# A lookup's gate matrices with their columns in one run, and the end of the kernel dealt with token block by token block

## The chip, the cores and the metric

The kernel runs on one NeuronCore of a Trainium2 chip. The metric is device time in microseconds (us) of one execution. Five engines with their own instruction queues work side by side and wait for one another by semaphores: TensorE (PE; its weight loads are shown apart as PEld), VectorE (DVE), ScalarE (ACT), GpSimd (POOL) and SyncE (SP), which here issues all loads. Tiles have 128 partitions; on-chip memory is SBUF, and matrix products are collected in PSUM.

## The reference

256 tokens of width 1024 pass a block of two layers and then a second block. Each layer of the first block has a mixer and a lookup feed-forward over 16384 small experts, a 128 by 128 grid. Cut to what matters:

```python
def peer(xn, w_q, sub_keys, u, v):                 # 256 tokens, 8 heads
    q = (t @ w_q).reshape(n_tok, 8, 2, 128)
    sc = jnp.einsum('thpd,hpnd->thpn', q, sub_keys)
    s1, i1 = lax.top_k(sc[:, :, 0], 16); s2, i2 = lax.top_k(sc[:, :, 1], 16)
    cand = s1[..., :, None] + s2[..., None, :]     # 16 x 16 candidates
    top_s, pos = lax.top_k(cand, 16)
    eidx = (i1 * 128 + i2) at pos                  # 8 x 16 = 128 picks per token
    gate = softmax(top_s)
    hid = gelu(einsum('td,thkd->thk', t, u[eidx]))
    return einsum('thk,thkd->td', gate * hid, v[eidx])
```

The second block ends in a mixture of 32 experts (four groups of eight, two of the eight chosen per token), a layer norm, a gated projection (`sigmoid(x @ ple_gate) * (p @ ple_proj)`) added to the residual stream, and a last layer norm.

## The kernel before, in words

A product of two fp32 matrices is made of three: each side is split into a high part (a cast on ACT) and a rest (a subtraction on DVE), both in a rounded fp32 format; hi·hi, lo·hi and hi·lo are added in PSUM. `split` (L98) does this, `wload` (L105) loads 128x1024 weights and splits them into `whi` and `wlo`, and `mm` (L119) issues every matmul.

The lookup does not gather. It computes the hidden value of every expert for every token and multiplies by a gate matrix that is zero except at the 128 picks of a token. `H[i2, i1, token]` holds it in three fp32 tiles (rows i1 0 to 63, 64 to 95, 96 to 127), each `[128, rows, 256]`, so that two neighbouring rows i1 of one token lie 1024 bytes apart. A loop over 128 rows i1 runs 24 matmuls `ph` each (8 x 3, moving 256 tokens), puts gelu(ph) into the row (tokens whose gate is already there are multiplied by it on DVE, L784; the others are written by ACT, L780), and from about the fortieth row on deals with groups of four tokens as its rate `due` allows: 64 groups spread over the remaining rows, so about two groups in three rows.

For one group, `build` makes two f16 tiles on DVE, with the 128 picks of a token on the partitions. `pab` holds two one-hot matrices (does pick k have i1 = n? i2 = n?) for four tokens, laid out `[128, 2, 128 values, 4 tokens]`: the token is the last index, so the 128 values of one token lie 8 bytes apart. `pgb` is the i2 one-hot times the gate, in a high and a low f16 part, in the same layout. Per token two matmuls follow (`gates`): the weights are a part of `pgb`, the moving side is the i1 one-hot, both read with that step of 8 bytes, and the sum of the two lands in 128 columns of a PSUM tile `g` of 512. Then `g` is taken out, one instruction for each of the three H tiles: rows with hidden values present are multiplied on DVE (L764, at the same time by 1/GATE_UNIT), the rest are written by ACT (L767); the elements go token by token and within a token along the rows.

What feeds `build` is `IT`, the transposed picks: two indices and the two gate parts, `[128, 4, 256]`, written once per layer by `to_picks` (L694 to L697) behind a search for the best sixteen on DVE. It runs over the first rows of the same loop.

The order on each engine is set by a scheduler that simulates the program, under pools of buffers; the helper `behind` adds an order dependence on one engine.

The last part: the 32 experts end with `ea` matmuls whose results are split into `yc` (L98). Then a branch runs an overflow path where a group has over 128 tokens; two numbers are read into registers ahead of it (`values_load`, L1537 and L1538), on every engine. Behind the branch, 32 `sc` matmuls put the experts' rows back in token order for the two token blocks t0 and t1, DVE adds the residual into `y` (L1552), and a layer norm (`Ln`) follows: statistics, a reciprocal root by a chain of small instructions (L167 to L182), two passes over the data (L317, L319), transposes `tp` (L204) and a split of what they give (`xh`, `xl`). Then `out_proj` runs 96 matmuls `o` against `ple_gate`, whose weights (`o00` to `o03`, `o10` to `o13`: half, quarter) are loaded and split behind the branch, and `sink` (L1584 to L1586), a last `Ln` and four stores end the program.

Of the kernel before, what the change touches and what calls it, by code (L numbers as in the profile page):

```python
# [8 lines left out]
F32 = mybir.dt.float32  # L9
# [44 lines left out]
def program(tc, A, out, stop=None, start=None):  # L54
# [16 lines left out]
    tinyp = ctx.enter_context(pool("tinyp", 3))  # L71
# [305 lines left out]
    def out_proj(wpool, src, xT, sink, order=(0, 1, 2, 3), both=1):  # L377
# [21 lines left out]
        for t in range(2):  # L399
            for n in range(2):  # L400
                for g in order[both:]:
                    if t == 0:
                        late[n, g] = wload(src[n, g], wpool, f"o{n}{g}")
                    block(late[n, g], g, n, t)
                sink(t, n, os_[t][n])
# [166 lines left out]
    def peer(l, xT, make):  # L572
        with ExitStack() as es:
# [4 lines left out]
            IT = pip.tile([P, 4, S], F16, tag="IT", name="IT")  # L578
            iota4 = pip.tile([P, P, 4], F16, tag="iota4", name="iota4")
            ACT.copy(iota4, iota[:, :, None].to_broadcast([P, P, 4]))  # L580
# [108 lines left out]
            def to_picks():  # L689
                for t in range(2):  # L690
# [4 lines left out]
                    ts = slice(t * P, (t + 1) * P)  # L695
                    V.tensor_copy(IT[:, 0:3, ts], ps[:, :384].rearrange("p (i t) -> p i t", i=3))
                    V.tensor_tensor(IT[:, 3, ts], ps[:, S:S + P], IT[:, 2, ts], op=ALU.subtract)  # L697

# [42 lines left out]
            def build(grp):  # L741
                ts = slice(4 * grp, 4 * grp + 4)
                ab = pw.tile([P, 2, P, 4], F16, tag="pab", name="pab", bufs=2)
                V.tensor_tensor(ab, iota4[:, None, :, :].to_broadcast([P, 2, P, 4]),  # L744
                                IT[:, 0:2, ts][:, :, None, :].to_broadcast([P, 2, P, 4]), op=ALU.is_equal)
                b = pw.tile([P, 2, P, 4], F16, tag="pgb", name="pgb", bufs=2)
                V.tensor_tensor(b, ab[:, 1:2, :, :].to_broadcast([P, 2, P, 4]),  # L747
                                IT[:, 2:4, ts][:, :, None, :].to_broadcast([P, 2, P, 4]), op=ALU.mult)
                built[grp] = ab, b

            def gates(grp, n):
                t0 = 4 * grp
                ab, b = built.pop(grp)
                ps = smt("g")
                for i in range(4):
                    for part in range(2):
                        mm(ps[:, i * P:(i + 1) * P], b[:, part, :, i], ab[:, 0, :, i], part == 0, part == 1)
                pv = ps.rearrange("p (t i) -> p t i", t=4)
                for o, end, part in parts:
                    size = end - o  # L760
                    hv = part[:, :, t0:t0 + 4].rearrange("p i t -> p t i")
                    m = min(max(n - o, 0), size)
                    if m:
                        V.scalar_tensor_tensor(hv[:, :, :m], hv[:, :, :m], 1.0 / GATE_UNIT, pv[:, :, o:o + m],  # L764
                                               op0=ALU.mult, op1=ALU.mult)
                    if m < size:
                        ACT.activation(hv[:, :, m:], pv[:, :, o + m:end], AF.Copy, scale=1.0 / GATE_UNIT)  # L767
# [61 lines left out]
            for t in range(2):  # L829
                for n in range(2):  # L830
                    for i1, w, v in held:
                        value_block(i1, w, v, t, (n,))
                    V.tensor_tensor(h[:, t, half(n)], h[:, t, half(n)], acc[t][n], op=ALU.add)
# [461 lines left out]
    def moe(x):  # L1295
        xT, (carry, (rs, rb, iota1), products), xn = x
        pp = ctx.enter_context(pool("pp")).tile([P, 2, D], F32, tag="pp", name="pp")
        with ExitStack() as es:
# [89 lines left out]
            wr = es.enter_context(pool("mwr", RAWS))  # L1388
# [50 lines left out]
            yc, accs = {}, {}  # L1439
# [10 lines left out]
            def overflow():  # L1450
# [27 lines left out]
                for e in range(8):  # L1478
                    pu = up(lambda q: A["exp_gu_g"][bass.ds(group, 1), e, q].rearrange("a p c -> (a p) c"),
                            [[x[:, k, :] for k in range(DK)] for x in xo])  # L1480
                    hT = middle(pu, co[:, e:e + 1])
                    down(lambda f: A["exp_down_g"][bass.ds(group, 1), e, f].rearrange("a p c -> (a p) c"),
# [43 lines left out]
            before = None  # L1526
# [220 lines left out]
```

## Time and profile before

| | us |
|---|---|
| three runs | 2632.81, 2632.82, 2633.84 |
| median | 2632.82 |
| the profiled execution's own time | 2631.19 |
| its span in the profile | 2629.4 |
| PE busy (matmul) | 2554.3 |
| DVE busy | 1929.9 |
| ACT busy | 1362.3 |

The page sums busy time over the whole program, so its shares are means over stages. The views beneath are read stage by stage: windows (busy time in a stretch), groups of instructions by shape (count, mean length), and timelines (start, length and count of neighbouring instructions of one kind). A matmul's length in a timeline reaches past the start of the next one, as they overlap in the array; what a matmul costs is the distance from start to start. The first lookup's gates stand between 305 and 621 us, the second's between 1254 and 1571 us, and the last part begins at about 2571 us.

### The profile page before, as it was taken

To read this page: it belongs to the slowest core of one execution; us is meant where nothing else is said; L and a number is where in the kernel's file an instruction comes from. 1 tells how busy PE (TensorE), PEld (TensorE's weight loads), DVE (VectorE), ACT (ScalarE), POOL (GpSimd) and SP (SyncE) were. 2 spreads that over 40 slices of the span, in tenths; PEclk is the share of its full clock that TensorE was granted. 3 is DMA by queue.
4 is the path that set the end of the run, shared out by engine and by line. 5 is a ranking of instruction groups with operands and counts; after the bars stand their busy time and mean duration, and the time that the engine had idled before them with its cause. 6 is when DMAs were issued, how large, how long until landed. Compare 5 with 4: busy or idle time off the path is not lost. (4 is left out here: it accounts for less than half of the span.)

```text
span 2629.4 us, 42151 instructions
## 1 busy us (share of the span) xinstructions
PE 2554.3 (97%) x16202; PEld 2288.0 (87%) x16202; DVE 1929.9 (73%) x3548; ACT 1362.3 (52%) x2315; POOL 3.3 (0%) x24
## 2 busy tenths in 40 slices
PE   8999999999999999999999999999999999899996
PEld 7899999998888889899999998888878899688885
DVE  6689877887555556799878885555567566799997
ACT  5555655444444444555554444444456433478872
POOL 0000000000000000000000000000000000000000
PEclk9999999999999999999999999999999999899998
DMA  6445444444555554555444445555644214599983
GB/s 210 162 137 184 163 151 149 152 150 161 191 186 190 186 200 152 172 167 184 148 150 153 153 149 182 190 186 195 205 162 132 77 61 142 204 351 351 353 320 113
DMA packets 131777, 474.74 MB, mean 181 GB/s; under 512 B 15218, under 2 KB 16242, under 8 KB 131314
## 3 DMA queue, kind: packets, MB, share of 16 engines
q1 hardware_dynamic: 131570, 472.00, 52.8%
q8 instruction: 128, 2.10, 0.3%
q14 instruction: 79, 0.65, 0.1%
HBM read 470.89 MB, written 1.05 MB: 179 GB/s over the span
## 5 line engine op out<-in xcount | busy, mean ns | idle before, releaser
L98 DVE TENSOR_TENSOR wlo<-raw,whi 128x1024 fp32r<-128x1024 f32 x738 | 902.1, 1223 | 512.3 <-ACT whi L98 481.1
L98 ACT CAST whi<-raw 128x1024 fp32r<-128x1024 f32 x738 | 775.2, 1051 | 871.1 <-PE acc L119 349.9
L119 PE MATMUL ph<-xh,whi 128*128 128x256 f32 x2048 | 511.8, 288 | 0.0
L119 PE MATMUL ph<-xl,whi 128*128 128x256 f32 x2048 | 501.4, 282 | 0.0
L119 PE MATMUL acc<-whi,hw 128*128 128x512 f32 x1952 | 496.5, 396 | 2.4 <-ACT hw L98 2.2
L119 PEld LDWEIGHTS acc<-whi,hw 128*128 128x128 f32 x1952 | 366.7, 188 | 91.9 <-ACT hw L98 2.6
L119 PEld LDWEIGHTS ph<-xh,whi 128*128 128x128 f32 x2048 | 392.6, 192 | 0.1
L119 PEld LDWEIGHTS ph<-xl,whi 128*128 128x128 f32 x2048 | 391.6, 191 | 0.0
L119 PE MATMUL ph<-xh,wlo 128*128 128x256 f32 x2048 | 287.2, 283 | 0.0
L119 PE MATMUL acc<-wlo,hw 128*128 128x512 f32 x976 | 267.9, 396 | 0.0
L119 PEld LDWEIGHTS ph<-xh,wlo 128*128 128x128 f32 x2048 | 264.1, 192 | 0.0
L119 PEld LDWEIGHTS acc<-wlo,hw 128*128 128x128 f32 x976 | 183.5, 188 | 44.2
L119 PE MATMUL g<-pab,pgb 128*128 128x128 f16 x1024 | 140.6, 296 | 0.0
L98 DVE TENSOR_TENSOR mlo<-raw,mhi 128x1024 fp32r<-128x1024 f32 x96 | 116.7, 1223 | 10.9 <-ACT mhi L98 8.1
L764 DVE SCALAR_TENSOR_TENSOR H<-H,g 128x256 f32<-128x256 f32 (+26 forms) x254 | 120.9, 515 | 0.5 <-PE g L119 0.4
L767 ACT ACTIVATE H<-g 128x128 f32<-128x128 f32 (+20 forms) x254 | 67.9, 360 | 99.5 <-DVE H L764 99.5
L98 ACT CAST mhi<-raw 128x1024 fp32r<-128x1024 f32 x96 | 100.9, 1053 | 25.1 <-PE gu L119 19.4
L119 PEld LDWEIGHTS <-pgb 128*128 128x128 f16 x1024 | 105.0, 118 | 6.5
L747 DVE TENSOR_TENSOR pgb<-pab,IT 128x1024 f16<-128x1024 f16 x128 | 87.5, 688 | 1.9
L744 DVE TENSOR_TENSOR pab<-iota,IT 128x1024 f16<-128x1024 f16 x128 | 87.2, 682 | 0.0
L98 DVE TENSOR_TENSOR hw<-H,hw 128x512 fp32r<-128x512 f32 x128 | 87.1, 684 | 0.0
L780 ACT ACTIVATE H<-ph 128x256 f32<-128x256 f32 (+40 forms) x254 | 78.2, 308 | 12.0 <-PE ph L119 11.9
(676 smaller groups left out, 3599.0 us busy)
## 6 DMA issues: line engine op xcount, KB each, us to landing
raw<-in_peer_u SPq DMA_DIRECT2D x256, 512.0 KB, 3.3
raw<-in_peer_v SPq DMA_DIRECT2D x256, 512.0 KB, 4.2
raw<-in_exp_gu SPq DMA_DIRECT2D x128, 512.0 KB, 5.3
raw<-in_exp_down SPq DMA_DIRECT2D x64, 512.0 KB, 5.2
raw<-in_peer_w_q SPq DMA_DIRECT2D x32, 512.0 KB, 3.3
raw<-in_even_w_in SPq DMA_DIRECT2D x28, 512.0 KB, 4.2
raw<-in_odd_w_in SPq DMA_DIRECT2D x24, 512.0 KB, 3.8
raw<-in_w_in_g SPq DMA_DIRECT2D x16, 512.0 KB, 3.3
```

What stands on the lines that cost most here:

```text
L98: return ACT.copy(hi, src), V.tensor_tensor(lo, src, hi, op=ALU.subtract)
L119: i = nc.tensor.matmul(o, l, r, start=start, stop=stop)
L744: V.tensor_tensor(ab, iota4[:, None, :, :].to_broadcast([P, 2, P, 4]), IT[:, 0:2, ts][:, :, None, :].to_broadcast([P, 2, P, 4]), op=ALU.is ...
L747: V.tensor_tensor(b, ab[:, 1:2, :, :].to_broadcast([P, 2, P, 4]), IT[:, 2:4, ts][:, :, None, :].to_broadcast([P, 2, P, 4]), op=ALU.mult)
L764: V.scalar_tensor_tensor(hv[:, :, :m], hv[:, :, :m], 1.0 / GATE_UNIT, pv[:, :, o:o + m], op0=ALU.mult, op1=ALU.mult)
L767: ACT.activation(hv[:, :, m:], pv[:, :, o + m:end], AF.Copy, scale=1.0 / GATE_UNIT)
L780: ACT.activation(hrow[:, tk:], ph[:, tk:S], AF.Gelu)
```

## The change

The gate side of the lookup is laid out token by token. `IT` becomes `[128, 64 groups, 4, 4 tokens, 2]` with each value stored twice, `iota4` becomes a plain row of 128 numbers, and `pab` is `[128, 2, 4 tokens, 128 values]`, so that a token's 128 columns are one run of 256 bytes. The gate now multiplies the i1 one-hot, the side that moves, and the weights are the bare i2 one-hot; there are still two products per token. The multiplication that made `pgb` is two instructions of 512 elements in place of one of 1024. `g` is taken out with rows as the outer and tokens as the inner index, so that H is touched in runs of four words and PSUM with a step of 512 bytes. The factor 1/GATE_UNIT moves to the add that ends the lookup. `to_picks` writes each value twice, by three copies and a subtraction of 256 elements per token block, in place of one copy of 384 and a subtraction of 128. Tiny tiles have two buffers in place of three.

In the last part the registers are loaded, in program order, ahead of expert (3, 0); the first two `ple_gate` weights (`a0`, `a1`) are loaded and split in front of the branch and the next two right behind it; the layer norm runs with `in_turn`, so that t1's residual add waits for t0's last pass; and `out_proj` takes those weights as they are.

```diff
@@ -68,7 +68,7 @@
     wp = ctx.enter_context(pool("wp", 2))
     hp = ctx.enter_context(pool("hp", 1))
     xp = ctx.enter_context(pool("xp", 1))
-    tinyp = ctx.enter_context(pool("tinyp", 3))
+    tinyp = ctx.enter_context(pool("tinyp", 2))
     mm_ps = ctx.enter_context(tc.tile_pool(name="mm_ps", bufs=2, space=PSUM))
     sm_ps = ctx.enter_context(tc.tile_pool(name="sm_ps", bufs=4, space=PSUM))
@@ -400,7 +400,7 @@
             for n in range(2):
                 for g in order[both:]:
                     if t == 0:
-                        late[n, g] = wload(src[n, g], wpool, f"o{n}{g}")
+                        late[n, g] = ready[n, g] if (n, g) in ready else wload(src[n, g], wpool, f"o{n}{g}")
                     block(late[n, g], g, n, t)
                 sink(t, n, os_[t][n])
@@ -575,9 +575,10 @@
             pw = es.enter_context(pool("pw", 4))
             pip = es.enter_context(pool("pi"))
             last = hbp.tile([P, 32, S], F32, tag="last", name="H")
-            IT = pip.tile([P, 4, S], F16, tag="IT", name="IT")
-            iota4 = pip.tile([P, P, 4], F16, tag="iota4", name="iota4")
-            ACT.copy(iota4, iota[:, :, None].to_broadcast([P, P, 4]))
+
+            IT = pip.tile([P, 64, 4, 4, 2], F16, tag="IT", name="IT")
+            iota1 = pip.tile([P, P], F16, tag="iota1", name="iota1")
+            ACT.copy(iota1, iota)
             h0es = ExitStack()
             h0p = h0es.enter_context(pool("h0"))
             mid = h0p.tile([P, 32, S], F32, tag="mid", name="H")
@@ -692,9 +693,12 @@
                     for i in range(3):
                         nc.tensor.transpose(ps[:, i * P:(i + 1) * P],
                                             res[:, i, t, :, :].rearrange("p h k -> p (h k)"), ident)
-                    ts = slice(t * P, (t + 1) * P)
-                    V.tensor_copy(IT[:, 0:3, ts], ps[:, :384].rearrange("p (i t) -> p i t", i=3))
-                    V.tensor_tensor(IT[:, 3, ts], ps[:, S:S + P], IT[:, 2, ts], op=ALU.subtract)
+                    o = IT[:, 32 * t:32 * t + 32]
+                    pv = [ps[:, i * P:(i + 1) * P].rearrange("p (g t) -> p g t", t=4)[:, :, :, None]
+                          .to_broadcast([P, 32, 4, 2]) for i in range(3)]
+                    for i in range(3):
+                        V.tensor_copy(o[:, :, i], pv[i])
+                    V.tensor_tensor(o[:, :, 3], pv[2], o[:, :, 2], op=ALU.subtract)
             steps = [first_level(t, c) for c in range(16) for t in range(2)]
             for t in range(2):
@@ -739,32 +743,36 @@
             built = {}
             def build(grp):
-                ts = slice(4 * grp, 4 * grp + 4)
-                ab = pw.tile([P, 2, P, 4], F16, tag="pab", name="pab", bufs=2)
-                V.tensor_tensor(ab, iota4[:, None, :, :].to_broadcast([P, 2, P, 4]),
-                                IT[:, 0:2, ts][:, :, None, :].to_broadcast([P, 2, P, 4]), op=ALU.is_equal)
-                b = pw.tile([P, 2, P, 4], F16, tag="pgb", name="pgb", bufs=2)
-                V.tensor_tensor(b, ab[:, 1:2, :, :].to_broadcast([P, 2, P, 4]),
-                                IT[:, 2:4, ts][:, :, None, :].to_broadcast([P, 2, P, 4]), op=ALU.mult)
-                built[grp] = ab, b
+
+
+                it = IT[:, grp].rearrange("p r t k -> p (r t) k")[:, :, None, :]
+                ab = pw.tile([P, 2, 4, P], F16, tag="pab", name="pab", bufs=2)
+                V.tensor_tensor(ab.rearrange("p r t (i k) -> p (r t) i k", k=2),
+                                iota1.rearrange("p (i k) -> p i k", k=2)[:, None, :, :].to_broadcast([P, 8, 64, 2]),
+                                it[:, 0:8].to_broadcast([P, 8, 64, 2]), op=ALU.is_equal)
+                g = pw.tile([P, 4, 2, P], F16, tag="pgb", name="pgb", bufs=2)
+                for r in range(2):
+                    V.tensor_tensor(g[:, :, r, :].rearrange("p t (i k) -> p t i k", k=2),
+                                    ab[:, 0].rearrange("p t (i k) -> p t i k", k=2),
+                                    it[:, 8 + 4 * r:12 + 4 * r].to_broadcast([P, 4, 64, 2]), op=ALU.mult)
+                built[grp] = ab, g
             def gates(grp, n):
+
                 t0 = 4 * grp
-                ab, b = built.pop(grp)
+                ab, g = built.pop(grp)
                 ps = smt("g")
                 for i in range(4):
-                    for part in range(2):
-                        mm(ps[:, i * P:(i + 1) * P], b[:, part, :, i], ab[:, 0, :, i], part == 0, part == 1)
-                pv = ps.rearrange("p (t i) -> p t i", t=4)
+                    for r in range(2):
+                        mm(ps[:, i * P:(i + 1) * P], ab[:, 1, i, :], g[:, i, r, :], r == 0, r == 1)
+                pv = ps.rearrange("p (t i) -> p i t", t=4)
                 for o, end, part in parts:
-                    size = end - o
-                    hv = part[:, :, t0:t0 + 4].rearrange("p i t -> p t i")
-                    m = min(max(n - o, 0), size)
-                    if m:
-                        V.scalar_tensor_tensor(hv[:, :, :m], hv[:, :, :m], 1.0 / GATE_UNIT, pv[:, :, o:o + m],
-                                               op0=ALU.mult, op1=ALU.mult)
-                    if m < size:
-                        ACT.activation(hv[:, :, m:], pv[:, :, o + m:end], AF.Copy, scale=1.0 / GATE_UNIT)
+                    hv = part[:, :, t0:t0 + 4]
+                    m = min(max(n, o), end)
+                    if m > o:
+                        V.tensor_tensor(hv[:, :m - o], hv[:, :m - o], pv[:, o:m], op=ALU.mult)
+                    if m < end:
+                        ACT.copy(hv[:, m - o:], pv[:, m:end])
             grp, due = 0, 0.0
             for i1 in range(NK):
@@ -830,7 +838,8 @@
                 for n in range(2):
                     for i1, w, v in held:
                         value_block(i1, w, v, t, (n,))
-                    V.tensor_tensor(h[:, t, half(n)], h[:, t, half(n)], acc[t][n], op=ALU.add)
+                    V.scalar_tensor_tensor(h[:, t, half(n)], acc[t][n], 1.0 / GATE_UNIT, h[:, t, half(n)],
+                                           op0=ALU.mult, op1=ALU.add)
                     if nxt:
                         nxt.half(t, n)
             return nxt.late() if nxt else None
@@ -1523,9 +1533,13 @@
                 V.tensor_copy(flag[:, 0:1], c8[:, 0:1])
                 V.tensor_copy(flag[:, 1:2], ci[:, 0:1])
-            before = None
+            before, vals = None, []
             for g in range(4):
                 for e in range(8):
+                    if (g, e) == (3, 0):
+                        vals += [nc.values_load(flag[0:1, 0:1], min_val=0, max_val=256),
+                                 nc.values_load(flag[0:1, 1:2], min_val=0, max_val=3)]
+                        nonlocal_group[:] = vals[1:]
                     pu = up(lambda q: A["exp_gu"][8 * g + e, q], [[x[:, k, g, :] for k in range(DK)] for x in xc])
                     if before is None:
                         with tc.issue_after(gathered.ins):
@@ -1534,24 +1548,32 @@
                         finish_expert(*before)
                     before = (e, g, middle(pu, cw[:, g, e:e + 1]))
             finish_expert(*before)
-            vals = nc.values_load(flag[0:1, 0:1], min_val=0, max_val=256), \
-                nc.values_load(flag[0:1, 1:2], min_val=0, max_val=3)
-            group = vals[1]
+
+            ahead = {}
+            for g in range(2):
+                raw = rawp.tile([P, 1024], F32, tag="raw", name="raw")
+                nc.sync.dma_start(raw, A["ple_gate"][0, g])
+                ahead[0, g] = [wr.tile([P, 1024], F32R, tag="raw", name=f"a{g}") for _ in range(2)]
+                split(raw, *ahead[0, g])
+            rooms[:] = [(0, rawp, "raw")] * 4
             with tc.If(vals[0] > P):
                 overflow()
+            for g in range(2, 4):
+                ahead[0, g] = wload(A["ple_gate"][0, g])
             gb_ = st([P, 2, D], "gb", tag="xc0")
             for i in range(2):
                 nc.sync.dma_start(gb_[:, i, :], A[f"lnr2{i}"].partition_broadcast(P))
-            ln = Ln([y[:, t, :] for t in range(2)], [gb_[:, i, :] for i in range(2)])
+            ln = Ln([y[:, t, :] for t in range(2)], [gb_[:, i, :] for i in range(2)], in_turn=True)
             for t in range(2):
                 for n in range(2):
                     ps = mmt("sc")
                     for g in range(4):
                         for i in range(2):
                             mm(ps, selT[:, g, t * P:(t + 1) * P], yc[g][i][:, half(n)], g == 0 and i == 0, g == 3 and i == 1)
-                    V.scalar_tensor_tensor(y[:, t, half(n)], h[:, t, half(n)], ALPHA, ps, op0=ALU.mult, op1=ALU.add)
+                    with behind(ln.done):
+                        V.scalar_tensor_tensor(y[:, t, half(n)], h[:, t, half(n)], ALPHA, ps, op0=ALU.mult, op1=ALU.add)
                     ln.half(t, n)
-            return ln.xT, pp
+            return ln.xT, pp, ahead, own
     def ple_products(ep):
```

On DVE, in the first lookup at rows i1 of about 93, a stretch of the loop read as follows before (`wlo` is the split of the loop's weights, `ge` the gelu of tokens already gated):

```order
L764 SCALAR_TENSOR_TENSOR H<-H,g 128x4x64
L764 SCALAR_TENSOR_TENSOR H<-H,g 128x4x29
L784 TENSOR_TENSOR H<-H,ge 128x160
L744 TENSOR_TENSOR pab<-iota_1365,IT 128x1024
L747 TENSOR_TENSOR pgb<-pab,IT 128x1024
L98 TENSOR_TENSOR wlo<-raw,whi 128x1024
L764 SCALAR_TENSOR_TENSOR H<-H,g 128x4x64
```

The same stretch now:

```order
L773 TENSOR_TENSOR H<-H,g 128x64x4
L773 TENSOR_TENSOR H<-H,g 128x29x4
L792 TENSOR_TENSOR H<-H,ge 128x160
L750 TENSOR_TENSOR pab<-iota_1365,IT 128x1024
L755 TENSOR_TENSOR pgb<-pab,IT 128x4x128 x2
L98 TENSOR_TENSOR wlo<-raw,whi 128x1024
L773 TENSOR_TENSOR H<-H,g 128x64x4
```

Nothing has moved there: one instruction of `pgb` has become two, and `H<-H,g` has rows outside and four tokens inside.

On PE, where the first gates of the first lookup begin (`it` is a transpose of `to_picks`), the rows before were the following:

```order
L119 MATMUL ph<-xl,whi 128x256
L119 MATMUL ph<-xh,wlo 128x256 x8
L119 MATMUL ph<-xh,whi 128x256
...
L119 MATMUL ph<-xl,whi 128x256
L119 LDWEIGHTS pgb
L119 MATMUL g<-pab,pgb 128x128
L119 LDWEIGHTS pgb
L119 MATMUL g<-pab,pgb 128x128
```

And now:

```order
L694 MATMUL it<-ident,H 128x128
L119 MATMUL ph<-xh,wlo 128x256 x8
L119 LDWEIGHTS pab
L119 MATMUL g<-pgb,pab 128x128
L119 MATMUL ph<-xh,whi 128x256
...
L119 MATMUL ph<-xl,whi 128x256
L119 LDWEIGHTS pab
L119 MATMUL g<-pgb,pab 128x128
L119 MATMUL ph<-xh,whi 128x256
L119 MATMUL ph<-xl,whi 128x256
L119 LDWEIGHTS pab
L119 MATMUL g<-pgb,pab 128x128
```

A single pair of a gate's weight load and matmul now stands ahead of the next row's 24 `ph` matmuls, a second one (of another group) within them, and the gates' roles as weights and moving side are exchanged.

On DVE behind the branch (the last part's layer norm) before, from the first residual add on:

```order
L1552 SCALAR_TENSOR_TENSOR y_24052<-h,sc 128x512
L300 BN_STATS lst<-y_24052 128x6
L1552 SCALAR_TENSOR_TENSOR y_24052<-h,sc 128x512
L300 BN_STATS lst<-y_24052 128x6
L303 BN_AGGR lmv<-lst 128x2
L1552 SCALAR_TENSOR_TENSOR y_24052<-h,sc 128x512
L312 TENSOR_SCALAR lv<-lmv 128x1
L317 SCALAR_TENSOR_TENSOR y_24052<-y_24052,lmv,gb 128x512 x2
L300 BN_STATS lst<-y_24052 128x6
L171 TENSOR_SCALAR rsi<-lv 128x1
L1552 SCALAR_TENSOR_TENSOR y_24052<-h,sc 128x512
```

And now:

```order
L1574 SCALAR_TENSOR_TENSOR y_24188<-h,sc 128x512
L300 BN_STATS lst<-y_24188 128x6
L98 TENSOR_TENSOR wlo<-raw,whi 128x1024
L1574 SCALAR_TENSOR_TENSOR y_24188<-h,sc 128x512
L98 TENSOR_TENSOR wlo<-raw,whi 128x1024
L300 BN_STATS lst<-y_24188 128x6
L303 BN_AGGR lmv<-lst 128x2
...
L317 SCALAR_TENSOR_TENSOR y_24188<-y_24188,lmv,gb 128x512 x2
L319 SCALAR_TENSOR_TENSOR h<-y_24188,lr,gb 128x512 x2
L1574 SCALAR_TENSOR_TENSOR y_24188<-h,sc 128x512 x2
L300 BN_STATS lst<-y_24188 128x6
```

Before, t1's adds and statistics stand between the steps of t0's norm. Now t0's norm runs to its end (L319), and t1's adds come behind it.

On PE the `o` matmuls of the two token blocks were mixed, behind all transposes:

```order
L119 MATMUL sc<-yc_26782,selT 128x512
L204 MATMUL tp<-ident,h 128x128 x16
L119 MATMUL o_27711<-o00hi,xh 128x512
L119 MATMUL o_27711<-o00hi,xl 128x512
L119 MATMUL o_27711<-o00hi,xh 128x512
L119 MATMUL o_27711<-o00hi,xl 128x512
L119 MATMUL o_27713<-o00hi,xh 128x512
L119 MATMUL o_27713<-o00hi,xl 128x512
```

Now t0's transposes are followed by t0's first half (24 matmuls) before those of t1:

```order
L119 MATMUL sc<-yc_26946,selT 128x512
L204 MATMUL tp<-ident,h 128x128 x8
L119 MATMUL o_27870<-a_26953,xh 128x512
L119 MATMUL o_27870<-a_26953,xl 128x512
...
L119 MATMUL o_27870<-wlo,xh 128x512 x2
L204 MATMUL tp<-ident,h 128x128 x8
L119 MATMUL o_27871<-o10hi,xh 128x512
L119 MATMUL o_27871<-o10hi,xl 128x512
```

The transposes of t1 have moved behind the 24 matmuls of t0's first half. The loads into registers, on the other hand, stand directly in front of the branch on PE, ACT and DVE as before.

## Rows read from the trace of the kernel before

**Rows 1.** The page: busy time by engine, and the granted clock in 40 slices.
```profile
PE 2554.3 (97%) x16202; PEld 2288.0 (87%) x16202; DVE 1929.9 (73%) x3548; ACT 1362.3 (52%) x2315; POOL 3.3 (0%) x24
...
PEclk9999999999999999999999999999999999899998
```

**Rows 2.** Windows in the two lookups; per engine busy us (count), granted clock, DMA share, GB/s.
```profile
300.00:400.00 100.00, 100.00 (x840) 99.04 (x839) 77.25 (x131) 53.02 (x147) 0.00 (x0) 1.00 0.44 148
...
500.00:600.00 100.00, 100.00 (x840) 98.93 (x839) 86.19 (x150) 43.10 (x105) 0.00 (x0) 1.00 0.45 152
1100.00:1200.00 100.00, 100.00 (x841) 100.00 (x841) 94.00 (x388) 52.03 (x83) 0.00 (x0) 1.00 0.53 173
```

**Rows 3.** Groups by shape, whole run: busy us, mean ns | idle before.
```profile
L119 PE MATMUL g<-pab,pgb 128*128 128x128 f16 x1024 | 140.6, 296 | 0.0
...
L119 PEld LDWEIGHTS <-pgb 128*128 128x128 f16 x1024 | 105.0, 118 | 6.5
...
L747 DVE TENSOR_TENSOR pgb<-pab,IT 128x1024 f16<-128x1024 f16 x128 | 87.5, 688 | 1.9
L744 DVE TENSOR_TENSOR pab<-iota,IT 128x1024 f16<-128x1024 f16 x128 | 87.2, 682 | 0.0
...
L764 DVE SCALAR_TENSOR_TENSOR H<-H,g 128x256 f32<-128x256 f32 x86 | 64.2, 746 | 0.0
...
L767 ACT ACTIVATE H<-g 128x128 f32<-128x128 f32 x132 | 46.7, 431 | 8.9 <-DVE H L764 8.9
```

**Rows 4.** Timeline of PE, 400 to 410 us: start, length, line, operation, count.
```profile
403.08 1.12 PE L119 MATMUL ph<-xh,wlo 128*128 128x256 f32 x8
404.05 1.11 PE L119 MATMUL g<-pab,pgb 128*128 128x128 f16 x8
404.91 0.37 PE L119 MATMUL ph<-xh,whi 128*128 128x256 f32 x1
```

**Rows 5.** Timeline of PE in the last part, idle before and what ended it.
```profile
2587.45 1.94 PE L204 MATMUL tp<-ident,h 128*128 128x128 f32 x8 [5.61 <-DVE h L319]
...
2598.58 0.40 PE L119 MATMUL o<-o01hi,xh 128*128 128x512 f32 x1
2598.81 0.40 PE L119 MATMUL o<-o01hi,xl 128*128 128x512 f32 x1
```

**Rows 6.** Timeline of PE, 2100 to 2106 us: full fp32 with 128 columns.
```profile
2103.52 1.05 PE L119 MATMUL i<-XT,it 128*128 128x128 f32 x8
2104.41 1.06 PE L119 MATMUL i<-it,XT 128*128 128x128 f32 x8
```

**Rows 7.** Timeline of weight loads, 402.5 to 405 us.
```profile
402.97 1.03 PEld L119 LDWEIGHTS ph<-xh,wlo 128*128 128x128 f32 x8
404.04 0.82 PEld L119 LDWEIGHTS <-pgb 128*128 128x128 f16 x8
```

**Rows 8.** Groups by shape on DVE, 300 to 640 us.
```profile
L764 DVE SCALAR_TENSOR_TENSOR H<-H,g 128x128 f32<-128x128 f32 x23 | 10.1, 438 | 0.2 <-PE g L119 0.2
...
L696 DVE CAST IT<-it 128x384 f16<-128x384 f32 x1 | 0.6, 558 | 0.1
...
L784 DVE TENSOR_TENSOR H<-H,ge 128x256 f32<-128x256 f32 x1 | 0.4, 420 | 0.0
L684 DVE TENSOR_TENSOR H<-H 128x512 bf16<-128x512 bf16 x1 | 0.4, 413 | 0.0
```

**Rows 9.** Lines 1343 (comparison that repeats one word) and 697: ns min/median/max.
```profile
L1343 DVE TENSOR_TENSOR sel<-iota,key x2: 673/682/692, 2279.1 to 2282.4; 128x512 fp32r<-128x512 f32 x2
...
L697 DVE TENSOR_TENSOR IT<-it,IT x4: 280/284/286, 298.0 to 1264.1; 128x128 f16<-128x128 f32 x4
```

**Rows 10.** Chain that ended last, in order of time: start, us, what.
```profile
2586.59 1.38 DVE h L319 x2
...
2592.49 24.92 PE o L119 x96
...
2619.41 1.41 DVE y L319 x2
```

More of the change, by code (lines that the diff above doesn't have):

```diff
@@ L375, in fresh, with out_proj @@
             return nxt.late()
-    def out_proj(wpool, src, xT, sink, order=(0, 1, 2, 3), both=1):
+    def out_proj(wpool, src, xT, sink, order=(0, 1, 2, 3), both=1, ready=()):
         os_ = [[mmt(f"o{t}{n}") for n in range(2)] for t in range(2)]
@@ L1387, in moe @@
             y = late.tile([P, 2, D], F32, tag="y2", name="y2")
-            wr = es.enter_context(pool("mwr", RAWS))
+            own = ExitStack()
+            wr = own.enter_context(pool("mwr", RAWS, side="right"))
             turn = [0]
@@ L1437, in down @@
                                first and f == 0 and i == 0, last and f == 1 and i == 2)
-            yc, accs = {}, {}
+            yc, accs, nonlocal_group = {}, {}, []
             def finish_expert(e, g, hT):
@@ L1478, in overflow @@
                 for e in range(8):
-                    pu = up(lambda q: A["exp_gu_g"][bass.ds(group, 1), e, q].rearrange("a p c -> (a p) c"),
+                    pu = up(lambda q: A["exp_gu_g"][bass.ds(nonlocal_group[0], 1), e, q].rearrange("a p c -> (a p) c"),
                             [[x[:, k, :] for k in range(DK)] for x in xo])
                     hT = middle(pu, co[:, e:e + 1])
-                    down(lambda f: A["exp_down_g"][bass.ds(group, 1), e, f].rearrange("a p c -> (a p) c"),
+                    down(lambda f: A["exp_down_g"][bass.ds(nonlocal_group[0], 1), e, f].rearrange("a p c -> (a p) c"),
                          hT, acc, e == 0, e == 7)
@@ L1575, in ple @@
     def ple(x):
-        xT, pp = x
+        xT, pp, ahead, own = x
         with pool("pl") as ep, pool("plo") as wo, pool("plw", 2) as ew:
@@ L1587, in sink @@
                 ln.half(t, n)
-            out_proj(wo, A["ple_gate"], xT, sink, both=0)
+            out_proj(wo, A["ple_gate"], xT, sink, both=0, ready=ahead)
+        own.close()
     def after(name, x):
@@ L1618, in program @@
                     evacuated[:] = split(h[:, t, :], *[a[:, t, :] for a in xn])
-            xT = (xT, pre, xn) if origin == "ln1" else (xT, pp)
+            xT = (xT, pre, xn) if origin == "ln1" else (xT, pp, {}, ExitStack())
         after(origin, xT)
```

## The prediction

> **What bounds the kernel now.** I read the page's busy line and the slices first: PE is busy 2554.3 of 2629.4 us at a granted clock of nine tenths or more in nearly every slice, DVE 73%, ACT 52% [rows 1]. So work that PE loses comes off the end, as long as nothing else becomes the bound there. [...] In 1100 to 1200 us, the search for the best picks, DVE is at 94.00 and PE still at 100.00: up to that share DVE does not hold PE up [rows 2]. Then the groups by shape: 1024 gate matmuls, with nothing idle ahead of them [rows 3]. Last the timelines, for what one of them costs.
>
> **The gate matmuls.** Eight of them last 1.11 us and one 0.296 [rows 3, 4], so one starts (1.11 − 0.296)/7 = 116 ns after the other. All 1024 take 119 us. The `ph` matmuls ahead of them move 256 columns and need (404.05 − 403.08)/8 = 121 ns each [rows 4]; those of the last part move 512 and need 230 ns [rows 5]. From 121 and 230, 128 columns should cost 121 − 109/2 = about 66 ns; in proportion to 256 it would be 60. Before, the 128 columns cost what 256 do. Two things may be the cause. One is the moving side's step of 8 bytes; the change takes it away. The other is the weight load. Full fp32 with 128 columns runs at (2104.41 − 2103.52)/8 = 111 ns [rows 6], which is close; but eight fp32 loads at a pitch of 121 ns end 1.03 us after the first began, so one lasts about 1.03 − 7 x 0.121 = 0.18 us, against 118 ns for one of f16 [rows 3, 7]: the f16 load should not need the room of an fp32 one. Both sides are contiguous now, so either cause goes unless the load has a price of its own. I take 64 ns: 1024 x (116 − 64) = 53 us less. Bounds from rows: 60 ns (57 us less) and 116 (nothing).
>
> [...]
>
> **What DVE pays per group.** `pab` stays one instruction of 1024 f16 elements (682 ns [rows 3]). Its operands now repeat pairs in place of running over four tokens; a comparison that repeats one word over 512 fp32 elements costs 682 ns [rows 9], much as any of that size, so I count nothing. The bounds are 0 and, if repeated pairs ran at half speed, +0.35 us. `pgb` goes from one instruction of 688 ns to two of 512 elements; 512 two-byte elements cost 413 [rows 8], so 2 x 413 − 688 = +0.14 us per group. Taking `g` out costs 746 ns for 256 elements and 438 for 128 [rows 3, 8], 2.41 ns an element, where the contiguous multiplication of `H` by `ge` needs 420 for 256 [rows 8]. H now comes in runs of four words, PSUM with a step of 512 bytes, which no row shows. The lower bound is 420; above there is no row that ends it, so I keep 746 (the nearest: same operands, one of them strided) and put the dearer case among the rivals. ACT's part (431 ns for 128 [rows 3]) lies on an engine half idle, and costs nothing up to twice that.
>
> [...]
>
> Does DVE still keep up? Three rows of `ph` and two groups make a period of 3 x 24 x 0.120 + 2 x 8 x 0.116 = 10.5 us; now 16 x 0.052 = 0.83 us less, 9.7. DVE in 500 to 600 us works 86.19% [rows 2], 9.05 us per period, plus 2 x 0.14 = 9.3: 96%, just above what was seen to be harmless. In 300 to 400 it is (8.1 + 0.3)/9.7 = 87%. So I count 4 us of small waits over the late half of both lookups.
>
> **The rest of the lookup.** `to_picks` per token block goes from 558 ns [rows 8] plus a subtraction of 284 [rows 9] to four instructions of 256 elements at 420: +0.84 us, four blocks in all, while DVE is near the 94% of rows 2; at worst 3.4 us, none if the search has slack. I take 1.5. The first runs of gates now have single pairs between `ph` matmuls of the row before; PE works in order, so if `pgb` of that group is late, all `ph` behind it wait. Before, the gates came in whole blocks later. A `pab` and a `pgb` last 1.4 us [rows 3]; with one such wait in each lookup that is about 2 us once part of it is hidden, bounds 0 and (two in each) 5. The final add by 1/GATE_UNIT is as long as the plain one: nothing. The third tiny buffer is used by no chain that runs beside two others here: nothing, or some tenths where a norm waits.
>
> **The last part.** The register loads have not moved in the executed order, so that edit is worth nothing. The two early weight splits lie under the last expert's `ea` matmuls, and so are hidden; without cover they would cost 2 x 1.05 us on ACT. `in_turn` makes t0's last pass end earlier: it stands at 2586.59 with two instructions of 0.69, behind t1's adds and statistics [rows 10]; about 2 us of those go from its way, and one weight split comes in. The first 24 `o` matmuls then need only t0's transposes, of which before the first began at 2587.45 behind 5.61 us of idle PE [rows 5], and the `o` began at 2592.49 [rows 10]. I put them at 2588. [...] The 96 `o` last 24.92 us [rows 10]; with t1's eight transposes (about 2) within, PE ends near 2615 in place of 2617.4. At the end, t0's last pass (1.41 us between t1's steps [rows 10]) is out of the way. Together −3 to −4; I take −3.5, bounds +1 (t1 late, PE idle again) and −6.
>
> **The sum.** −53 + 4 + 1.5 + 2 − 3.5 = −49 us. From the profiled execution's own 2631.2 that is 2582; its time lies 1.6 us below the runs' median of 2632.8, so against the median 2583.8. I say 2583.
>
> **The rivals.**
> 1. *DVE becomes the bound in the late half.* If taking out `g` costs 3.3 ns an element rather than 2.41 (or `pab` and `pgb` slow by 0.35 us each), a period late gets about 0.7 us longer on DVE (2 x 0.35, or some 720 elements x 0.9 ns), 10.0 against PE's 9.7; where DVE is heaviest nearly half the gain goes, and hiccups grow elsewhere. Some 20 us of the 53 return: 2605. For it: no row prices a PSUM step of 512 bytes; DVE stands at 96% even in my own sum. Against it: H gets friendlier than in the 746 row.
> [...]
> 3. *Slower: DVE's read of PSUM costs so much that it paces the whole lookup.* On the mean over both lookups DVE has about 8.5 + 0.3 us of work per period, some 575 of the elements taken out among it. It reaches the old 10.5 us at 2.41 + 1.7/0.575 = 5.4 ns an element; at 6.4, each of the 60 periods or so takes 0.6 us more than before, 35 us in all: 2665. Its place is the instruction on L773 (512 bytes from element to element); 5.4 ns is where it decides. For it: nothing but the missing row. Against it: the dearest step in these rows is 2.41.
> 4. *The last part does not gain* (t1's norm late behind the splits): +4 on the forecast, within its range.
>
> **How the numbers follow.** Forecast with its own range of 2571 to 2594: 0.68. Rival 1 (2594 to 2615): 0.16. Rival 2: 0.10, half of it below 2612. Rival 3: 0.05. Below 2571: in the rest. The range 2570 to 2612 leaves out rival 3, half of rival 2 and the ends. What a measurement can tell from no change is 0.2%, 5.3 us: faster 0.91 (forecast, rival 1, most of rival 2), same 0.04 (the rest of rival 2), slower 0.05.
>
> **What would show it.** Right: eight gate matmuls in about 0.75 us in place of 1.11; PE still at 100 in 300 to 600 us; each lookup about 25 us shorter; two `pgb` of about 0.41 us; `o` starting near 2588 minus the shift, and t1's transposes between `o`s with little idle time. [...]

## The result and the profile after

The changed kernel takes 2571.07 us in the median of four runs (2569.51 to 2573.53), against 2633.32 before (2632.81 to 2633.84): 62 us less, a ratio of 0.976 with an interval of 0.975 to 0.978. The prediction was 2583 with a range of 2570 to 2612. The profiled execution of after took 2573.53 us with a span of 2571.8; against the profiled one of before (2631.19) that is 57.7 us less.

The groups by shape (count, busy us, mean ns | idle before) that answer to [rows 3]:

```profile
L755 DVE TENSOR_TENSOR pgb<-pab,IT 128x512 f16<-128x512 f16 x256 | 96.1, 419 | 1.9
L750 DVE TENSOR_TENSOR pab<-iota,IT 128x1024 f16<-128x1024 f16 x128 | 87.3, 683 | 0.0
L119 PE MATMUL g<-pgb,pab 128*128 128x128 f16 x1024 | 80.1, 220 | 0.0
...
L119 PEld LDWEIGHTS <-pab 128*128 128x128 f16 x1024 | 58.1, 98 | 5.7
...
L773 DVE TENSOR_TENSOR H<-H,g 128x256 f32<-128x256 f32 x86 | 35.6, 414 | 0.0
...
L775 ACT COPY H<-g 128x128 f32<-128x128 f32 x132 | 31.1, 275 | 8.3 <-DVE H L773 8.3
```

One gate matmul is shown with 220 ns in place of 296, its weight load with 98 in place of 118. Taking out 256 elements costs DVE 414 ns in place of 746, and ACT's 128 elements 275 in place of 431. `pab` stands where it stood (683), and `pgb` is two of 419.

The timeline of PE (start, length, line, operation, count), answering to [rows 4]:

```profile
401.25 0.62 PE L119 MATMUL g<-pgb,pab 128*128 128x128 f16 x8
...
404.63 0.62 PE L119 MATMUL g<-pgb,pab 128*128 128x128 f16 x8
```

Eight gate matmuls last 0.62 us: (0.62 − 0.22)/7 = 57 ns from start to start, where it was 116. A row with one group takes 404.63 − 401.25 = 3.38 us; before, such a row took 3.82 (gates from 1566.38 to 1570.20). That is 0.44 us for eight, or 55 ns each. The 59 ns by which the step fell would give 0.47 for eight.

The windows of the lookups (per engine busy us and count, granted clock, DMA share, GB/s), answering to [rows 2]:

```profile
300.00:400.00 100.00, 100.00 (x922) 98.93 (x921) 82.52 (x174) 54.19 (x160) 0.00 (x0) 1.00 0.50 167
500.00:590.00 90.00, 90.00 (x821) 89.23 (x821) 77.69 (x169) 41.23 (x104) 0.00 (x0) 1.00 0.50 165
```

PE is still busy all the time, at a granted clock of 1.00. DVE's share is no higher than before late in the lookup (77.69 of 90 is 86.3%), though the same work now stands in less time: what taking out `g` gave back pays for that.

The length of a lookup is read from its first `ph` matmul to the first `acc` matmul behind it, before:

```profile
195.00 0.36 PE L119 MATMUL ph<-xh,whi 128*128 128x256 f32 x1
...
625.92 2.08 PE L119 MATMUL acc<-whi,hw 128*128 128x512 f32 x6 [1.08 <-ACT hw L98]
```

and after:

```profile
195.40 0.36 PE L119 MATMUL ph<-xh,whi 128*128 128x256 f32 x1
...
598.66 1.19 PE L119 MATMUL acc<-whi,hw 128*128 128x512 f32 x4 [1.08 <-ACT hw L98]
```

It took 430.9 us before and takes 403.3; the second went from 430.9 to 403.3 too. So the two lookups give 55.2 us. The rest of the 57.7 lies in the last part. Its start on PE before (in square brackets, here and below, stand the idle time of the engine and what ended it):

```profile
2571.15 0.61 PE L119 MATMUL ea<-mlo,hh 128*128 128x512 f32 x2
2574.08 1.20 PE L119 MATMUL sc<-yc,selT 128*128 128x512 f32 x4 [2.32 <-DVEq L1540]
```

and after:

```profile
2516.39 0.61 PE L119 MATMUL ea<-mlo,hh 128*128 128x512 f32 x2
2519.85 10.42 PE L119 MATMUL sc<-yc,selT 128*128 128x512 f32 x32 [2.84 <-PEq L1559]
2533.57 1.94 PE L204 MATMUL tp<-ident,h 128*128 128x128 f32 x8 [3.30 <-DVE h L319]
2535.33 0.80 PE L119 MATMUL o<-a,xh 128*128 128x512 f32 x1
2536.52 0.79 PE L119 MATMUL o<-a,xl 128*128 128x512 f32 x1 [0.40 <-DVE xl L98]
...
2543.28 1.04 PE L204 MATMUL tp<-ident,h 128*128 128x128 f32 x8
```

And some steps of the chain that ended last there (start, us, what), answering to [rows 10]:

```profile
2519.34 5.26 DMA raw<-in_ple_gate
...
2525.79 0.80 DVE wlo L98
...
2527.61 1.14 DVE wlo L98
...
2532.76 1.32 DVE h L319 x2
...
2544.32 16.73 PE o L119 x72
```

From the end of the last `ea` matmul (2517.0) to the end of the span it takes 54.8 us; before, it took 57.6 (2571.8 to 2629.4). I call this time the stretch. The 24 `o` matmuls of t0's first half now stand between the two blocks of transposes. But the rests of two weight splits (`wlo`, 0.80 and 1.14 us of it) lie on the chain in the middle of t0's norm, behind a wait for the load of the first, and the `o` matmuls go on only 19.5 us after the last `ea` (they began 20.7 behind it before).

The stretch itself is not the same in every execution. Five runs below have the last part of the change as it stands (`moving_step`, `weights_step`, `tail_only`, `old_evac`, `evac_pad`); their profiled executions show 53.1, 55.1, 54.8, 55.1 and 54.2 us. In all six t0's last pass ends 15.7 to 17.1 us after the last `ea`, and the `o` matmuls go on 18.2 to 19.5 after it. In `gates_only`, which has the last part of before, the stretch is 57.3. So the gain of the last part is clear of this spread (2.2 us at the least), but differences of 2 us or less between single traces are not.

### The profile page after: what moved, and what is told of

Its sections match the earlier page's. It is cut to its first block, busy times and chain, and to the rows that moved or that the text cites. A ratio compares the mean times of both kernels' runs of the same rounds, so it can differ in the third digit from the quotient of the medians.

```text
span 2571.8 us, 42289 instructions
## 1 busy us (share of the span) xinstructions
PE 2500.3 (97%) x16202; PEld 2234.9 (87%) x16202; DVE 1892.0 (74%) x3684; ACT 1346.5 (52%) x2315; POOL 3.2 (0%) x24
## 5 line engine op out<-in xcount | busy, mean ns | idle before, releaser
L755 DVE TENSOR_TENSOR pgb<-pab,IT 128x512 f16<-128x512 f16 x256 | 96.1, 419 | 1.9
L775 ACT COPY H<-g 128x128 f32<-128x128 f32 (+20 forms) x254 | 48.2, 243 | 79.8 <-DVE H L773 79.8
L119 PE MATMUL g<-pgb,pab 128*128 128x128 f16 x1024 | 80.1, 220 | 0.0
L98 ACT CAST hw<-H 128x512 fp32r<-128x512 f32 x128 | 78.4, 617 | 0.0
L773 DVE TENSOR_TENSOR H<-H,g 128x256 f32<-128x256 f32 (+26 forms) x254 | 71.2, 314 | 5.6 <-PE g L119 5.6
```

Source lines behind the costliest of these rows:

```text
L98: return ACT.copy(hi, src), V.tensor_tensor(lo, src, hi, op=ALU.subtract)
L119: i = nc.tensor.matmul(o, l, r, start=start, stop=stop)
L755: V.tensor_tensor(g[:, :, r, :].rearrange("p t (i k) -> p t i k", k=2), ab[:, 0].rearrange("p t (i k) -> p t i k", k=2), it[:, 8 + 4 * r:1 ...
L773: V.tensor_tensor(hv[:, :m - o], hv[:, :m - o], pv[:, o:m], op=ALU.mult)
L775: ACT.copy(hv[:, m - o:], pv[:, m:end])
```

## The experiments

**Which step cost the 116 ns?** Two kernels are the changed one but for one operand of the gate matmuls, read with a step of 8 bytes out of the same tile (so the gates' values are others).

```diff
-  mm(..., ab[:, 1, i, :], g[:, i, r, :], ...)
+  mm(..., ab[:, 1, i, :], g.rearrange("p t r (j s) -> p (t r j) s", s=4)[:, P*r:P*r+P, i], ...)   # moving_step
+  mm(..., ab.rearrange("p r t (j s) -> p (r t j) s", s=4)[:, P*r:P*r+P, i], g[:, i, r, :], ...)   # weights_step
```

> The changed kernel, but the gate matmuls read their moving columns with a step of 8 bytes out of the same tile (other columns, so the gates hold other values; the weights stay contiguous). Theory (the moving side's step set the 116 ns from start to start): eight gate matmuls last 1.1 us again, about 57 us come back, some 2628 us; the weight load stays at 98 ns. Rival (the step on the weight load set it): eight in 0.62 us, 2571 us.

> The changed kernel, but the weights of the gate matmuls are read with a step of 8 bytes (other values; the moving side stays contiguous). Theory (moving side): the weight load grows from 98 to about 118 ns but eight matmuls still take 0.62 us, 2571 us. Rival (weight load): eight in 1.1 us, some 2628 us. If both are stepped reads that cost, each by itself gives the full 57 us.

Measured: 2624.4 us (2623.2 to 2627.0) with the moving side stepped, 2571.1 (2568.7 to 2573.4) with the weights stepped. The groups of the first, and eight of its gate matmuls in a timeline:

```profile
L119 PE MATMUL g<-pgb,pab 128*128 128x128 f16 x1024 | 138.6, 292 | 0.0
...
L119 PEld LDWEIGHTS <-pab 128*128 128x128 f16 x1024 | 102.3, 111 | 5.6
...
403.37 1.08 PE L119 MATMUL g<-pgb,pab 128*128 128x128 f16 x8
```

and of the second:

```profile
L119 PE MATMUL g<-pgb,pab 128*128 128x128 f16 x1024 | 82.5, 223 | 0.0
...
L119 PEld LDWEIGHTS <-pab 128*128 128x128 f16 x1024 | 62.3, 116 | 5.7
...
402.17 0.64 PE L119 MATMUL g<-pgb,pab 128*128 128x128 f16 x8
```

With the step on the moving side the matmul is back at 292 ns (296 before), one starts (1.08 − 0.29)/7 = 113 ns after the other, and both lookups take 429.9 us each, 27 more. With the step on the weights the load goes from 98 to 116 ns, the matmul stays at 223, the distance is (0.64 − 0.22)/7 = 60 ns, and a lookup takes 404.9 us, 1.6 more. So nearly all of the 55 us (53.3 by itself) is the moving side's, and about 3 the weights'. The rival is out. (In the first, the weight load is shown with 111 ns although its operand was contiguous; no run shows why.)

**The two halves of the change apart.** `gates_only` is the kernel before with the lookup's part and the two tiny buffers, which belong to the larger `IT`. `tail_only` is the kernel before with the rest.

> The kernel before with the lookup's part of the change alone (and the two tiny buffers that it needs), the last part as before. Theory: the two lookups give 55 us and the last part 3: 2574 to 2575 us, 3 above the changed kernel. Rival (the last part gives nothing, its reordering is hidden or paid back by its longer sc matmuls): 2571 us, as the changed kernel.

> The kernel before with the last part's changes alone. Theory: 3 us less than before, 2630 us, t0's first 24 o matmuls starting some 4 us earlier after the last ea matmul than before and t1's norm beneath them. Rival (nothing): 2633 us.

Measured: 2573.4 us (2571.3 to 2579.2) and 2628.1 (2624.9 to 2630.5; ratio to before 0.997 to 0.999). Whole times move by several us from execution to execution (see the end), so I read the stretch: from the last `ea` to the end 57.3 us in `gates_only`, 54.8 in `tail_only`, against 57.6 before and 54.8 after. A lookup takes 403.3 us in `gates_only` and 430.9 in `tail_only`, as after and before, so the two parts are independent. The last part gives 2.5 to 2.8 us in these traces.

**Does DVE's load cost PE anything?** `old_evac` takes `g` out in the old order (token by token), with the new matmuls.

```diff
-  pv = ps.rearrange("p (t i) -> p i t", t=4);  hv = part[:, :, t0:t0 + 4]
+  pv = ps.rearrange("p (t i) -> p t i", t=4);  hv = part[:, :, t0:t0 + 4].rearrange("p i t -> p t i")
```

> The changed kernel, but g is taken out in the old order (token by token, H touched with a step of 1024 bytes, PSUM contiguous). Theory of the prediction (at the old price DVE stands at 96% and costs PE about 4 us of waits): some 746 ns for 256 elements again, DVE at 93 to 97 of 100 us late in the lookups, the two lookups together 2 to 5 us longer than in the changed kernel, 2574 to 2576 us. Rival (DVE's load does not matter below 100%): lookups as long as in the changed kernel, 2571 us. Rival (DVE becomes the bound): 20 us longer, 2591 us.

Measured: 2569.6 us (2567.4 to 2573.7). The price is back, and DVE is fuller:

```profile
L773 DVE TENSOR_TENSOR H<-H,g 128x256 f32<-128x256 f32 x86 | 64.3, 748 | 0.0
```

The last window of the lookup in `old_evac`:

```profile
500.00:590.00 90.00, 90.00 (x826) 89.18 (x824) 87.03 (x168) 41.74 (x106) 0.00 (x0) 1.00 0.50 164
```

DVE is at 87.03 of 90, or 96.7%, and each lookup takes 403.3 us, as with the cheap form. The term of 4 us is refuted, and so is the idea behind it: a share of 94% was only the highest that the trace of before had shown, not a limit. `evac_pad` is `old_evac` with one more DVE instruction per group (each `pab` made twice):

> The kernel with g taken out in the old order, and each pab made twice (the second time over the first, the same values): one more DVE instruction of 680 ns per group, 0.61 us from start to start. Theory (DVE holds PE up only where its work exceeds PE's time): DVE's work in 300 to 590 us goes from 262.5 to about 301 us against 290 of PE, so each lookup gets 10 to 15 us longer than 403 us, 20 to 30 in both; 2590 to 2600 us, PE waiting for pgb or for ph's buffers. Rival (waits begin earlier and add up, as the prediction's 4 us assumed): 40 us or more. Rival (there is still room): within 5 us of 2570.

Measured: 2595.1 us (2594.0 to 2596.2), and each lookup 413.7 us, 10.5 more:

```profile
300.00:400.00 100.00, 98.76 (x896) 96.74 (x895) 95.72 (x183) 55.70 (x155) 0.00 (x0) 1.00 0.49 160
400.00:500.00 100.00, 100.00 (x907) 98.47 (x906) 99.44 (x189) 51.32 (x135) 0.00 (x0) 1.00 0.50 163
500.00:600.00 100.00, 99.70 (x893) 97.91 (x892) 100.00 (x192) 48.30 (x113) 0.00 (x0) 1.00 0.48 159
```

Now DVE is the bound: it reaches 99.44 and 100.00, and the time follows its work (some 301 us forecast where PE needs 290, 11 more). PE is shown busy for 98 to 100 us of 100 all the same; it holds fewer matmuls (893 in the last window, where the change has 821 in 90 us). A PE that is "busy" all the time is thus no proof that PE is the bound; DVE's own share and the count of matmuls decide.

**What gives the 2.8 us of the last part?** `turn_only` drops the early weights and keeps the norm in turn; `early_only` drops the turn. The edits, shortened:

```diff
-  ahead[0, 0..3] loaded and split around the branch        # turn_only: ahead = {}
-  ln = Ln(..., in_turn=True)                               # early_only: ln = Ln(...)
```

> The changed kernel without the ple_gate weights ahead of the branch and right behind it: the norm in turn is left. Theory (the turn gives the gain): the two weight splits that stand in t0's norm are gone, t0's h about 1 us earlier, but the first o matmuls wait for a split behind t1's norm on DVE only for their rests; the stretch from the last ea matmul to the end 54 to 56 us (57.6 before, 54.8 after). Rival (the early weights give it): 57 us or more, because the o matmuls wait for their weights.

> The changed kernel without the turn: weights ahead of the branch as in the change, the two token blocks' norms mixed as before. Theory (the turn gives the gain): the stretch from the last ea matmul to the end 57 us, as before. Rival (the early weights give it): 55 us.

Measured: 2575.0 us (2573.0 to 2577.7) and 2573.9 (2570.6 to 2575.5); the stretch is 59.4 and 56.9 us. PE in `turn_only`:

```profile
2513.64 0.61 PE L119 MATMUL ea<-mlo,hh 128*128 128x512 f32 x2
...
2527.78 1.29 PE L204 MATMUL tp<-ident,h 128*128 128x128 f32 x8 [1.91 <-DVE h L319]
2535.86 1.97 PE L204 MATMUL tp<-ident,h 128*128 128x128 f32 x8 [6.80 <-DVE h L319]
2537.48 0.78 PE L119 MATMUL o<-o00hi,xh 128*128 128x512 f32 x1
```

t0's transposes come 3 us earlier than in the change (13.5 us after the last `ea` against 16.6), but the scheduler puts no `o` matmul between them and t1's; PE waits 6.80 us for t1's norm. The `o` matmuls' weights are split only behind t0's transposes there. PE in `early_only`:

```profile
2515.00 0.61 PE L119 MATMUL ea<-mlo,hh 128*128 128x512 f32 x2
...
2536.16 1.94 PE L204 MATMUL tp<-ident,h 128*128 128x128 f32 x8 [8.94 <-DVE h L319]
2537.92 0.80 PE L119 MATMUL o<-a,xh 128*128 128x512 f32 x1
2538.51 1.30 PE L204 MATMUL tp<-ident,h 128*128 128x128 f32 x8
```

Here both norms end late (8.94 us idle). Both theories fall: against the 57.6 of before the turn alone loses 1.8 us and the early weights alone win 0.7, and only together they give 2.8. With one trace of each, neither the 1.8 nor the 0.7 is clear of the spread of 2 us; that neither edit alone reaches the 53.1 to 55.1 us of both is. The turn makes a gap, and the weights, being there, let 24 matmuls into it.

**The weight rest in t0's norm.** `late_split` splits the two weights behind the branch only behind t0's last pass, `late_split2` only behind t0's `xl`. The edits, shortened:

```diff
-  for g in range(2, 4): ahead[0, g] = wload(A["ple_gate"][0, g])   # right behind the branch
+  if t == 0:                                   # in the loop over t, behind ln.half(0, 1)
+      for g in range(2, 4):
+          ahead[0, g] = wload(A["ple_gate"][0, g], behind=(ln.done, ln.done))   # late_split2: behind the splits of t0's xT
```

> The changed kernel with the two weight loads behind the branch split only behind t0's last pass (in the change one of the two rests stands in the middle of t0's norm). Theory: t0's last pass 1.1 to 1.8 us earlier after the last ea matmul, t1's later by 1, the stretch to the end 53.5 to 54 us in place of 54.8. Rival (the rests now stand ahead of t0's xl and hold the o matmuls up instead): 54.8 or more.

Measured: 2569.4 us (2568.4 to 2570.4), the stretch 55.3. DVE behind t0's norm:

```profile
2525.57 1.28 DVE L1572 SCALAR_TENSOR_TENSOR y<-h,sc 128x512 f32<-128x512 f32 x2
2526.76 1.22 DVE L98 TENSOR_TENSOR wlo<-raw,whi 128x1024 fp32r<-128x1024 f32 x1
...
2528.50 1.21 DVE L98 TENSOR_TENSOR wlo<-raw,whi 128x1024 fp32r<-128x1024 f32 x1
...
2530.23 1.27 DVE L98 TENSOR_TENSOR xl<-tp,xh 128x512 fp32r<-128x512 f32 x2
```

t0's last pass ends 14.05 us after the last `ea` (17.07 in the change), 3.0 earlier, but the two rests now stand ahead of `xl`, and the `o` matmuls go on 19.4 us after it, as in the change. That is the rival: a wait was moved, not removed.

> The changed kernel with the two weight loads behind the branch split on DVE only behind t0's xl, so that they stand neither in t0's norm nor ahead of the first o matmuls. Theory (t0's norm and xl are the chain there): the first o matmul 15 us after the last ea matmul, the second not before 16 (18.3 and 19.5 in the changed kernel), and the stretch from the last ea matmul to the end 52 to 53.5 us in place of 54.8; 2569 us. Rival (t1's norm, now 2 us later, leaves PE idle ahead of its transposes): 54.8 again.

Measured: 2571.2 us (2569.9 to 2571.7), the stretch 52.5. PE in it:

```profile
2516.85 0.61 PE L119 MATMUL ea<-mlo,hh 128*128 128x512 f32 x2
2519.78 9.29 PE L119 MATMUL sc<-yc,selT 128*128 128x512 f32 x32 [2.32 <-DVEq L1559]
2530.99 1.29 PE L204 MATMUL tp<-ident,h 128*128 128x128 f32 x8 [1.92 <-DVE h L319]
2532.29 0.50 PE L119 MATMUL o<-a,xh 128*128 128x512 f32 x1
2533.95 0.80 PE L119 MATMUL o<-a,xl 128*128 128x512 f32 x1 [1.16 <-DVE xl L98]
...
2541.17 1.32 PE L204 MATMUL tp<-ident,h 128*128 128x128 f32 x8
```

The `o` matmuls go on 16.5 us after the last `ea`, 3.0 earlier than in the change, and the stretch is 2.3 shorter, as expected; it is 0.7 below the shortest of the six traces with the change's last part. The whole time is not the 2569 us expected. PE is idle for only 0.1 us ahead of t1's transposes.

`warm2` is `late_split2` with eight matmuls, whose sum nothing reads, on PE between the last `ea` and the branch:

```diff
+  busy(8, mm_last[0])            # behind the last expert; 8 x mm(ps, selT[:, 0, 0:P], yc[0][0][:, half(0)], True, True)
```

> The same with eight more matmuls of 512 columns, whose sum nothing reads, put on PE between the last ea matmul and the branch, where PE was idle for 2.3 us. Theory (PE falls to its lower clock level in that gap and the 32 sc matmuls pay for it): 32 sc in 7.5 us in place of 9.3, the stretch to the end 1 to 1.5 us shorter than without them. Rival (the clock does not depend on that gap, or the branch waits for the added matmuls): no gain or 1 us more.

Measured: 2569.8 us (2565.3 to 2571.9), the stretch 51.4. PE in it:

```profile
2511.67 2.03 PE L119 MATMUL gu<-yc,selT 128*128 128x512 f32 x8
2514.66 7.73 PE L119 MATMUL sc<-yc,selT 128*128 128x512 f32 x32 [0.96 <-PEq L1567]
```

The 32 `sc` take 7.73 us in place of 9.29, and the idle time ahead of them shrinks to 0.96, though they begin 0.5 later. The granted clock over them is 1.00 (2514.6 to 2522.4 us), where in `late_split2` it is 0.82 (2519.7 to 2529.1), behind an idle time of 2.32 us. Part of the gain is paid back by the later start; 1.1 us are left. That the added matmuls kept the clock up is likely but not shown: the kernel before, without them, also stood idle 2.32 us there, and its 32 `sc` took 7.76 us at a granted clock of 1.00. By the stretch this is the shortest version, 3.4 us ahead of the change; by whole times (ratio to before 0.975 to 0.978, that of the change 0.975 to 0.978) it cannot be told from it.

## Why the prediction held, point by point

- *The gate matmuls*: forecast 64 ns by a line through 121 and 230 ns, measured 57; −53 us forecast, −55.2 for the lookups as a whole. The mechanism was right, and `moving_step` shows that the moving side's step was the cause. That the size came so close is in part luck: the prediction counted 1024 full steps, which with the 57 ns would have given 60 us, and a step too long by 7 ns made up for it. The rival of the weight load or the pair (rival 2 in the chances) is out: the trace has 57 ns with a weight load for every matmul. Half of that rival's chance stands below 2612 us, for a pace between the forecast's 64 ns and the 111 of full fp32; no run shows one, the gate matmuls came 57 or 60 ns apart, or 113 or 116.
- *What DVE pays*: `pab` 683 (nothing forecast), `pgb` 2 x 419 (413 forecast). Taking out `g` was mis-sized. I kept 746 ns for 256 elements; it is 414, the lower bound, which is what the contiguous multiplication cost [rows 8]. A step of 512 bytes in PSUM, with runs of four words in H, costs nothing here (414 ns against 420); the steps in H were what cost 746 (`old_evac`, with PSUM contiguous and H stepped: 748).
- *DVE's small waits*, +4 us: did not come, and would not have come at the old price either (`old_evac`). The step that failed is "96%, just above what was seen to be harmless": `old_evac` lost nothing at 96.7%, and in `evac_pad` the time is close to what DVE's work needs, so the limit lies between.
- *`to_picks` and the first single gate pairs*, +3.5 us: from the first `ph` to the first gate it took 110.1 us before and takes 109.4 now (109.4 in the second lookup too). The first gates also stand earlier in the order now, so this alone would not show a loss under 1 us. But 1024 times 55 ns would give 56.3 us, and the lookups gave 55.2: by that sum about 1 us is left for the two.
- *The last part*: −3.5 forecast, −2.8 measured. The size was about right, the way to it was not. The prediction counted one weight split in t0's way; there were two, and the first of them waited for its load. So t0's last pass did not get earlier (17.1 us after the last `ea`, 16.2 before). Not all of that is the change: the 32 `sc` ahead of it ran at a granted clock of 0.72 after and 1.00 before, and in `gates_only`, at 0.83, the old last part had this pass at 17.6. The `o` matmuls began at 18.3 and went on at 19.5, not at 16.2 as forecast. What is left of it is 1.2 us (19.5 for 20.7). The other 95 `o` take 24.5 us from there with t1's transposes among them, 0.4 less than the 24.9 of all 96 without them before [rows 10] (granted clock 0.94 after, 0.90 before), and the end behind the last `o` went from 12.0 to 10.7 us, as t0's last pass is out of the way (1.4 forecast). The upper bound of +1, PE idle again with t1 late, did not come: t0's 24 `o` reach from 2535.33 to 2543.28 us (granted clock 0.74), and t1's transposes follow without idle time.
- *The sum*: −55.2 and −2.8 are −58.0, against 57.7 between the two profiled executions. The forecast of −49 was 9 short: 2 in the matmuls, 7.5 in waits that did not come, less 0.7 in the last part. The other 4.6 us of the 62 between the medians are no part of the change that I could find: the profiled execution was the slowest of the four of after, 2.5 us above their median, and that of before was 2.1 below its own. The 2571 us measured lie only 1 us inside the forecast's lower end of 2570, so the range held narrowly.

## What to carry to other kernels

When a matmul of few columns costs as much as one of twice as many, look at the step of its moving operand: reading 128 2-byte columns 8 bytes apart took twice as long as reading them in one run (113 and 116 ns against 57), while the same step on the weights hardly showed (60). No other step or element size was tried. DVE, which works beside the bound, could be filled to 96.7% here (`old_evac`) without costing anything; at 99 to 100% (`evac_pad`) the time followed its work, and the busy share of the waiting PE (98 to 100%) did not show it. And two edits may be worth nothing or less alone, because one opens a gap and the other fills it; try them apart before crediting either.

## What the runs showed of the hardware

The same instructions took a different time in different executions, longer where the granted clock was lower (0.90 against 1.00 here). One part of the second block (matmuls `pw` to `pl`, with 206 PE instructions) in the profiled execution of after, and under it in that of before:

```profile
1955.00:1990.00 35.00, 31.13 (x206) 25.74 (x204) 25.57 (x41) 13.93 (x24) 0.39 (x4) 0.90 0.41 128
```

```profile
2011.00:2043.00 32.00, 28.19 (x206) 23.51 (x205) 25.39 (x42) 13.93 (x24) 0.40 (x4) 1.00 0.44 141
```

In the first the clock is at 0.90 on the mean and this part takes 3 us longer than with 1.00 in the second (33.3 against 30.3 us from the first `pw` to the last), although the work is the same. PE stood idle for 2.3 us ahead of one `pw` in both; behind it the granted clock was 0.50 from 1969.4 to 1976.2 us in the first and stayed at 1.00 in the second. Likewise the 32 `sc` matmuls took 7.8 us before (granted clock 1.00), 10.4 after (0.72), and 9.2 or 9.3 in the others (0.82 or 0.83) but for `warm2`. So a change of a few us to this kernel is better read from a part of the trace than from whole times, and even there only beside the spread that the same code shows (53.1 to 55.1 us for the stretch). Whole times in one set of nine runs of the kernel before went from 2627.5 to 2636.1 us.
